# Expert loads in the order of use, and the branch to the general path ahead of the last two units

## The chip, the cores and the metric

The kernel runs on one core of a Trainium2 chip. The metric is the device time of one execution in microseconds. A core has engines that run their own instruction streams and wait for each other by semaphores: TensorE (PE, with PEld for its weight loads), VectorE (DVE), ScalarE (ACT), GpSimd (POOL) and SyncE (SP), which here issues every load from HBM. TensorE's granted clock has two levels, 1.2 and 2.4 GHz; the profile gives its mean as a share of the higher one.

## The reference

Two transformer blocks of two layers each work on 256 tokens of width 1024. Each layer is a token mixer and then a mixture of experts with 32 experts, of which every token uses two: first the best of four groups, then the two best of its eight experts. Cut to what matters, for block 1 (`D_EXPERT` is 512; in block 2 it is 256 and a layer norm takes the place of the gate):

```python
def hier_moe(h, wg, bg, we, be, w1, w3, w2):
    ...                                   # router: two experts and two weights per token
    xb = xt[buf_tok].reshape(nblk, MOE_BLOCK, d)   # tokens gathered by expert
    def expert_block(args):
        xi, e = args
        hid = jax.nn.silu(xi @ w1[e]) * (xi @ w3[e])
        return hid @ w2[e]
    yb = lax.map(expert_block, (xb, blk_exp)).reshape(p_rows, d)
    return zeros.at[buf_tok].add(yb * buf_w[:, None])
x = x + mixer(norm(x))
x = x + gt_f * hier_moe(modulate(norm(x)), ...)
```

All 32 experts' weights are read in every layer, in float32.

## The kernel before, in words

The program is one straight list of instructions, traced in Python; a scheduler then puts them in an order on each engine by its own costs and by the dependencies, and the result is fixed when the program is built. There are four expert stages: two in block 1 (`centred` false in the function `moe`) and two in block 2 (`centred` true), each behind a mixer.

In a stage the experts are taken in 11 units: five of two experts with room for 64 tokens each, five of four experts with room for 32, and a last one of two. The first 4 (block 1) or 6 (block 2) experts have fixed places; the rest is ordered by how many tokens chose them, so their weights' addresses are known only when the router is done. SP reads the order into a register (`TENSOR_LOAD kidx`, L726).

For each unit, with the names of the trace:
- `s<-w,xg` (L981): the gathered tokens `xg` times the joined w1 and w3 (tensor A), eight blocks k of the inner dimension. In block 1 a unit does this in two steps, half of its experts each.
- `hid` (L986, L987): SiLU on ACT, product on DVE; transposed on PE (L998) and copied by ACT to `ht` (L1000).
- `s<-w,ht` (L905, function `second`): `hid` times w2 (tensor B), for output half 0 and then half 1.
- `yh`, `yl` (L907 on ACT, L908 on DVE): the result in two parts for two cheaper products.
- `y<-yh,PT` and `y<-yl,PT` (L918, function `combine`): adds to the tokens' sums in PSUM. `back` prepares `PT`.
- `ms<-P,x` (L851): gathers the next group's tokens.

Weights pass through a ring of slots of 128 x 2048 float32, 1 MB each, filled by SP (L170). In block 1 the ring has 13 slots and 9 more during the expert stage; in block 2 it has 13 and 5. An expert takes four slots for A and two for B in block 1, two for A and one for B in block 2. A load may start when the products that read the slot's old contents are done. In before a unit's experts come one after the other, each with all its parts; then come the B parts. A product over block k needs the part with that k of every expert of its step; `second` of half 0 needs only the first half of each B.

A general path (`overfull`) stands for the case that an expert has more tokens than room. It is behind a branch on a count (`tc.If`, L740, its register loads on L965) and is not taken in these runs. No instruction traced behind the branch runs ahead of it on any engine, and SP waits there until its outstanding loads have landed. In before the branch stands inside the last unit. The path adds its result straight into `x` (block 1) or into `keep`, the residual sum (block 2). `residual` makes `keep`: in block 1 the gate row, in block 2 the sum of x and the scaled residual by four DVE operations (L1895, L1896) that need two `lnp` loads.

Of the kernel before, what the change touches and what calls it, by code (L numbers as in the profile page):

```python
# [28 lines left out]
E = 32  # L29
CAP = 64  # L30
# [21 lines left out]
class Core:  # L52
# [124 lines left out]
    def slot(self, src, shape):  # L177


        n = int(np.prod(shape[1:]))  # L180
        parts = -(-n // SLOT)
        m = n // parts
        views = []
        for i in range(parts):
            v = self.scratch()[:, :m]
            d = self.load(v, src[:, i * m:(i + 1) * m])
            if self.ordered:
                self.loaded = d.ins
            views.append(v.rearrange("p (a b) -> p a b", b=shape[2]) if len(shape) == 3 else v)
        return Blocks(views, shape) if parts > 1 else views[0]  # L190


class Blocks:
# [591 lines left out]
def moe(c, ctx, index, scale, shift, w13, w2, nf, spare, centred, residual, end):  # L785
# [150 lines left out]
    def experts(unit):  # L936
        e0, ne, _ = unit
        return [e0 + i if e0 < fixed else ranks.expert(e0 + i) for i in range(ne)]

    for g, us in enumerate(groups):  # L940
        if g:
            P, xg = nxt[:2]
        nxt = group(groups[g + 1], False) if g + 1 < len(groups) else (None, None, [])
        share = -(-len(nxt[2]) // len(us))
        for unit in us:
            e0, ne, cap = unit
            j = e0 - us[0][0]
            last = unit is units[-1]
            todo = [nxt[2].pop(0) for _ in range(min(share, len(nxt[2])))]
            pr = {"n": units.index(unit), "unit": unit, "h": []}  # L950
            who = experts(unit)
            if last:

                room, hT, keep = [c.scratch(), c.scratch()], c.scratch(), c.scratch()
                hT = hT.rearrange("p (a b) -> p a b", b=256)
                out, gate = residual(mp, keep, room)
                c.ordered = True
                slots = [w13(e) for e in who]
                pr["w2"] = [w2(e) for e in who]
                c.loaded, c.ordered = None, False  # L960
            pr["yh"] = p.tile([128, 2, 512], F32R, name="yh", tag="yy", bufs=2)
            pr["yl"] = p.tile([128, 2, 512], F32R, name="yl", tag="yy", bufs=2)

            def spare_path():
                n = nc.values_load(cnt[0:1, 0:1], min_val=0, max_val=E * CAP,  # L965
                                   skip_runtime_bounds_check_because="counts of tokens")
                overfull(c, sp, None if centred else c.tok, scale, shift, out, w, pos, n, nf, *spare, gate, room, hT, ranks)

            if last and centred:
                second(prev, 0)  # L970
                spare_path()
            per = ne // steps_of
            for u in range(steps_of):
                ws = slots[u * per:u * per + per] if last else [w13(e) for e in who[u * per:u * per + per]]
                q = sp.tile([128, 512], F32, name="s1")
                for k in range(8):
                    for i in range(128 // cap):

                        m, o = (i, 0) if centred else (i // 2, i % 2)
                        e = j + u * per + m  # L980
                        d = nc.tensor.matmul(q[cap * i:cap * i + cap, :], xg[:, k, e * cap:(e + 1) * cap],  # L981
                                             ws[m][:, k, 512 * o:512 * o + 512], start=k == 0, stop=k == 7)
                        if last and u == steps_of - 1 and k == 0:
                            c.loaded = d.ins
                hid = p.tile([128, 256], F32, name="hid", bufs=2)
                nc.scalar.activation(hid, q[:, 0:256], AF.Silu)  # L986
                nc.vector.tensor_mul(hid, hid, q[:, 256:512])  # L987
                half = len(todo) // 2
                for f in todo[:half] if u == 0 else todo[half:]:
                    f()  # L990
                if last and not centred and u == 0:
                    back(pr, j)
                    combine(prev)
                elif centred and prev is not None and not last:
# [7 lines left out]
                if last and not centred and u == 0:  # L1002
                    spare_path()
            if not last:
                pr["w2"] = [w2(e) for e in who]
            if centred:
                for f in todo[half:]:
                    f()
                if prev is not None:
                    second(prev, 1)  # L1010
                back(pr, j)
                if prev is not None:
                    combine(prev)
            elif not last:
                back(pr, j)
                second(pr, 0)
                if prev is not None:
                    combine(prev)
                second(pr, 1)
            prev = pr  # L1020
    c.table(second(prev, 0))
    combine(prev, (0,))
    second(prev, 1, "s1")
    combine(prev, (1,))
    end(room, keep, y)
    c.less(extra)


# [829 lines left out]
def experts_1(c, l):  # L1858

    nc, x = c.nc, c.x  # L1860
    with ExitStack() as ctx:
        def residual(mp, keep, room):
# [3 lines left out]
            return x, keep[:, 0:1024]  # L1866

        a1 = c.a["A1"][l].rearrange("(q i) p (k c) -> q i p k c", i=2, c=1024)
        b1 = c.a["B1"][l].rearrange("(q i) p (h f c) -> q i f p h c", i=2, h=2, f=4)

        def w1_of(pr, i, j, f):
            o = (f // 2) * 512 + j * 256 + (f % 2) * 128
            return a1[bass.ds(pr, 1), i, :, :, o:o + 128].rearrange("q p k c -> p (q k) c")

        def w2_of(pr, i, f):
            return b1[bass.ds(pr, 1), i, f].rearrange("q p h c -> p (q h) c")

        def end(room, gate, y):
            for hf in range(2):
                for t in range(2):  # L1880
                    o = (2 * t + hf) * 512
                    d = room[0][:, o:o + 512]
                    nc.vector.tensor_mul(d, y[t][hf], gate[:, hf * 512:hf * 512 + 512])
                    nc.vector.tensor_add(x[:, t, hf * 512:hf * 512 + 512], x[:, t, hf * 512:hf * 512 + 512], d)
        moe(c, ctx, l, c.gain, c.mod[:, l, 24:32], lambda e: c.slot(expert(c.a["A1"][l], e), [128, 8, 1024]),
            lambda e: c.slot(expert(c.a["B1"][l], e), [128, 2, 2048]), 512, (w1_of, w2_of), False, residual, end)


def residual_2(c, lnp, l, which, out):
# [9 lines left out]
def experts_2(c, l):  # L1899

    nc, x = c.nc, c.x
    with ExitStack() as ctx:
        a2 = c.a["A2"][l].rearrange("(q i) p (k c) -> q i p k c", i=2, c=512)
        b2 = c.a["B2"][l].rearrange("(q i) p (h f c) -> q i f p h c", i=2, h=2, f=2)

        def w1_of(pr, i, j, f):
            o = j * 256 + f * 128
            return a2[bass.ds(pr, 1), i, :, :, o:o + 128].rearrange("q p k c -> p (q k) c")

        def w2_of(pr, i, f):  # L1910
            return b2[bass.ds(pr, 1), i, f].rearrange("q p h c -> p (q h) c")

        def residual(mp, keep, room):
# [7 lines left out]
        moe(c, ctx, 2 + l, c.vec("lnc")[:, o:o + 8], c.vec("lnc")[:, o + 8:o + 16],  # L1921
            lambda e: c.slot(expert(c.a["A2"][l], e), [128, 8, 512]),
            lambda e: c.slot(expert(c.a["B2"][l], e), [128, 2, 1024]), 256, (w1_of, w2_of), True, residual, end)


def last(c, p, l, keep, y):
# [314 lines left out]
```

## Time and profile before

| | |
|---|---|
| three runs | 2489.33 us median (2487.82 to 2495.08) |
| profiled execution | 2492.49 us, span 2490.7 us |
| busy: PE, PEld, DVE, ACT, POOL | 2145.9, 1235.4, 882.3, 752.5, 41.5 us |
| moved by DMA | 775.10 MB, mean 311 GB/s |
| loads `w<-A`, `w<-B` | 384 and 192 of 1024.0 KB |
| mean granted clock | 0.927 |

The times come from three runs, the rows from one profiled execution. The span is from the first to the last instruction. Busy shares are means over mixers and expert stages, which have different limits, so the windows by stage are to be read instead: one row gives the busy time of each engine in a stretch, the clock, the share of the 16 DMA engines and the rate. The four expert stages lie at about 297 to 773, 947 to 1421, 1694 to 1951 and 2226 to 2477 us. In a timeline the bracket says how long the engine was idle and what ended that.

### The profile page before, as it was taken

The numbers are of one execution on the slowest core, as the hardware profiler recorded it, in microseconds if no ns is written. First come the engines' busy times: TensorE is split into PE (matmuls) and PEld (weight loads), VectorE is DVE, ScalarE is ACT, GpSimd is POOL, SyncE is SP. The second block draws the span as 40 slices with busy tenths as digits, with TensorE's granted clock in tenths as the row PEclk, the third lists the DMA queues.
The fourth block names the chain that finished last, engine by engine and source line by source line (L and its number), as shares of the span: only waits on it lengthen the run. The fifth ranks groups of instructions, "written<-read, shape, count | busy, mean of one in ns | idle before, by whom it ended". The sixth has DMA issues, their size and how long they took to land. (4 is left out here: it accounts for less than half of the span.)

```text
span 2490.7 us, 32411 instructions
## 1 busy us (share of the span) xinstructions
PE 2145.9 (86%) x12546; PEld 1235.4 (50%) x12546; DVE 882.3 (35%) x1979; ACT 752.5 (30%) x1493; POOL 41.5 (2%) x46
## 2 busy tenths in 40 slices
PE   7998899966668989997666699998987899999976
PEld 4667544322225864442221287994432678964322
DVE  3865511100003752111000254973111547851203
ACT  4642322211114451121111254562221445632211
POOL 0001000000001200000000000000000000000000
PEclk8999999988888998999888899998998889989998
DMA  9976669999997355999999951555899724557995
GB/s 394 402 279 263 252 272 401 421 421 421 421 421 309 120 235 186 402 412 421 421 421 422 390 200 58 200 188 231 344 422 418 316 87 139 187 193 288 422 420 228
DMA packets 110627, 775.10 MB, mean 311 GB/s; under 512 B 13161, under 2 KB 14569, under 8 KB 18042
## 3 DMA queue, kind: packets, MB, share of 16 engines
q1 hardware_dynamic: 110458, 772.85, 77.2%
q8 instruction: 106, 1.74, 0.3%
q14 instruction: 63, 0.52, 0.1%
HBM read 771.75 MB, written 1.05 MB: 310 GB/s over the span
## 5 line engine op out<-in xcount | busy, mean ns | idle before, releaser
L981 PE MATMUL s<-w,xg 128*32 128x512 f32 (+1 forms) x3072 | 603.2, 644 | 101.2 <-DMA w<-A 91.7
L905 PE MATMUL s<-w,ht 128*32 128x512 f32 (+1 forms) x1536 | 339.4, 663 | 64.1 <-DMA w<-B 63.1
L981 PEld LDWEIGHTS s<-w,xg 128*32 128x32 f32 (+1 forms) x3072 | 143.8, 127 | 410.5 <-issue 250.4
L369 PE MATMUL pj<-hi,wh 128*128 128x256 f32 x864 | 244.1, 285 | 3.4 <-ACT sg L1771 2.3
L370 PE MATMUL pj<-lo,wh 128*128 128x256 f32 x864 | 243.4, 283 | 0.0
L371 PE MATMUL pj<-hi,wl 128*128 128x256 f32 x864 | 240.6, 284 | 0.0
L908 DVE SCALAR_TENSOR_TENSOR yl<-s,ws,yh 128x512 fp32r<-128x512 f32 x88 | 66.0, 750 | 471.8 <-ACT yh L907 468.1
L905 PEld LDWEIGHTS s<-w,ht 128*32 128x32 f32 (+1 forms) x1536 | 84.4, 128 | 240.8 <-issue 142.5
L364 ACT ACTIVATE wh<-w 128x512 fp32r<-128x512 f32 x248 | 154.2, 630 | 120.0 <-PE pj L370 87.6
L907 ACT ACTIVATE yh<-s,ws 128x512 fp32r<-128x512 f32 x88 | 60.5, 688 | 419.4 <-PE s L905 405.8
L365 DVE TENSOR_TENSOR wl<-w,wh 128x512 fp32r<-128x512 f32 x248 | 167.2, 688 | 50.2 <-ACT wh L364 44.9
L987 DVE TENSOR_TENSOR hid<-hid,s 128x256 f32<-128x256 f32 x66 | 27.7, 420 | 439.1 <-ACT hid L986 439.1
L369 PEld LDWEIGHTS pj<-hi,wh 128*128 128x128 f32 x864 | 165.8, 192 | 10.5 <-ACT sg L1771 2.8
L986 ACT ACTIVATE hid<-s 128x256 f32<-128x256 f32 x66 | 25.4, 384 | 478.0 <-PE s L981 477.7
L371 PEld LDWEIGHTS pj<-hi,wl 128*128 128x128 f32 x864 | 164.4, 192 | 4.5 <-issue 1.4
L370 PEld LDWEIGHTS pj<-lo,wh 128*128 128x128 f32 x864 | 166.2, 192 | 0.7 <-issue 0.7
L332 DVE TENSOR_TENSOR wl<-w,wh 128x512 fp32r<-128x512 f32 (+2 forms) x164 | 112.6, 695 | 99.2 <-ACT wh L331 82.6
L331 ACT ACTIVATE wh<-w 128x512 fp32r<-128x512 f32 (+2 forms) x164 | 99.8, 614 | 115.1 <-PE pj L317 58.0
L851 PEld LDWEIGHTS ms<-P,x 128*128 128x128 f32 x640 | 80.6, 190 | 62.6 <-ACT xg L859 32.0
L859 ACT ACTIVATE xg<-ms,mod,gain 128x128 f32<-128x128 f32 x160 | 72.1, 458 | 125.4 <-PE ms L851 124.8
L317 PE MATMUL pj<-wl,hi 128*128 128x512 f32 (+2 forms) x272 | 106.9, 394 | 0.0
L316 PE MATMUL pj<-wh,hi 128*128 128x512 f32 (+2 forms) x272 | 102.2, 404 | 3.0 <-ACT rt L385 1.6
(636 smaller groups left out, 2723.9 us busy)
## 6 DMA issues: line engine op xcount, KB each, us to landing
w<-A SPq DMA_DIRECT2D x384, 1024.0 KB, 19.7
w<-B SPq DMA_DIRECT2D x192, 1024.0 KB, 19.7
w<-ada SPq DMA_DIRECT2D x48, 1024.0 KB, 9.1
w<-wi SPq DMA_DIRECT2D x48, 1024.0 KB, 8.6
w<-w SPq DMA_DIRECT2D x26, 1024.0 KB, 15.1
w<-wo SPq DMA_DIRECT2D x16, 1024.0 KB, 5.2
w<-wbr SPq DMA_DIRECT2D x8, 1024.0 KB, 5.0
w<-wi SPq DMA_DIRECT2D x4, 840.0 KB, 4.8
```

What stands on the lines that cost most here:

```text
L316: nc.tensor.matmul(qs[t][:, :n], a, wh[:, :n], start=s, stop=False)
L317: nc.tensor.matmul(qs[t][:, :n], a, wl[:, :n], start=False, stop=False)
L331: nc.scalar.activation(wh[:, :n], w[:, k], AF.Copy)
L332: nc.vector.tensor_sub(wl[:, :n], w[:, k], wh[:, :n].bitcast(F32))
L364: nc.scalar.activation(wh, w[:, k], AF.Copy)
L365: nc.vector.tensor_sub(wl, w[:, k], wh.bitcast(F32))
L369: nc.tensor.matmul(d, wh[:, e], hi, start=k == 0 and ch % 2 == 0, stop=False, skip_group_check=True)
L370: nc.tensor.matmul(d, wh[:, e], lo, start=False, stop=False, skip_group_check=True)
L371: nc.tensor.matmul(d, wl[:, e], hi, start=False, stop=k == nk - 1, skip_group_check=True)
L851: nc.tensor.matmul(q, src[i][:, t, k * 128:(k + 1) * 128], P[:, t, :m], start=start and t == 0, stop=stop and t == 1, skip_group_check=True)
L905: nc.tensor.matmul(q[cap * i:cap * i + cap, :], ht[:, o * cap:o * cap + cap], pr["w2"][i][:, half, f * 512:f * 512 + 512], start=f == 0, s ...
L981: d = nc.tensor.matmul(q[cap * i:cap * i + cap, :], xg[:, k, e * cap:(e + 1) * cap], ws[m][:, k, 512 * o:512 * o + 512], start=k == 0, sto ...
```

## The change

Three things are done in `moe`; line numbers of the changed kernel are 27 to 47 higher in the parts quoted.

First, `slots` replaces `slot` for the experts: the parts of all experts of a step are loaded in turn, part 0 of each, then part 1 of each. For B the two output halves come in turn in the same way. In block 2, where a B fits one slot with both halves, two experts' pieces of the same half now share a slot, as two DMAs of 512 KB; and a unit's B is loaded behind the next unit's A (`outer(prev, ...)`).

Second, the branch and its preparations stand at the unit `turn = len(units) - 2`, behind the loads of that unit's first step. In block 2 the unit before is finished completely ahead of it (`second` twice and `combine`).

Third, in block 1 the general path adds into a slot of its own (`held`, zeroed by GpSimd), which two DVE additions add to `x` in the last two units. `keep` and `held` are taken out of the ring.

```diff
+    def slots(self, srcs, shape):
+        n = shape[1] * shape[2]
+        parts = -(-n // SLOT)
+        views = [[] for _ in srcs]
+        for i in range(parts if parts > 1 else shape[1]):
+            for j, src in enumerate(srcs):
+                if parts > 1:
+                    v, m = self.scratch(), SLOT
+                else:
+                    m = shape[2]
+                    if j % (SLOT // m) == 0:
+                        room = self.scratch()
+                    v = room[:, j % (SLOT // m) * m:(j % (SLOT // m) + 1) * m]
+                d = self.load(v, src[:, i * m:(i + 1) * m])
...
+    def hold(self, pools):
+        pool = next(r for r in self.rings if r in pools)
+        self.rings.remove(pool)
+        return pool.tile([128, SLOT], F32, name="w")
...
+    def first(who, u):
+        per = len(who) // steps_of
+        return c.slots([w13(e) for e in who[u * per:u * per + per]], [128, 8, 512 if centred else 1024])
+    def outer(pr, who):
+        pr["w2"] = c.slots([w2(e) for e in who], [128, 2, 4 * nf])
+    turn = len(units) - 2
...
+            if n == turn:
+                if centred and prev is not None:
+                    outer(prev, experts(prev["unit"]))
+                    second(prev, 0)
+                    second(prev, 1)
+                    combine(prev)
+                    prev = None
+                keep = c.hold(extra)
+                held = None if centred else c.hold(extra)
+                begun = first(who, 0)
+                room, hT = [c.scratch(), c.scratch()], c.scratch()
+                out, gate = residual(mp, keep, room, held)
+                count = nc.values_load(cnt[0:1, 0:1], min_val=0, max_val=E * CAP,
+                                       skip_runtime_bounds_check_because="counts of tokens")
+                overfull(c, sp, None if centred else c.tok, scale, shift, out, w, pos, count, nf, *spare, gate, room,
+                         hT, ranks)
...
-                ws = slots[u * per:u * per + per] if last else [w13(e) for e in who[u * per:u * per + per]]
+                ws = begun if begun is not None and u == 0 else first(who, u)
...
-                if last and not centred and u == 0:
-                    spare_path()
-            if not last:
-                pr["w2"] = [w2(e) for e in who]
+            if last and not centred:
+                for t in range(2):
+                    nc.vector.tensor_add(c.x[:, t], c.x[:, t], out[:, t])
...
+    if centred:
+        outer(prev, prev["who"])
     c.table(second(prev, 0))
     combine(prev, (0,))
     second(prev, 1, "s1")
     combine(prev, (1,))
-    end(room, keep, y)
+    end(held, keep, y)
```

SP's list at the end of the first stage, before: the last unit's A and B loads, the branch, then the next mixer's loads (`A1` and `B1` are the weights of block 1, the numbers are slots in the order in which they are taken).

```order
L170 DMA w_4698<-A1 128x2048
...
L170 DMA w_4700<-B1 128x2048
...
L170 DMA w_4706<-B1 128x2048
L965 TENSOR_LOAD rcnt_2662
L740 COMPARE_AND_BRANCH
...
L740 UNCONDITIONAL_BRANCH
L170 DMA w_5286<-w1b 128x128
```

The same place in the changed kernel: eight A loads of the tenth unit, the branch, and behind it the rest of that unit and all of the last, then the mixer's loads.

```order
L170 DMA w_4453<-A1 128x2048
L1004 TENSOR_LOAD rcnt_2662
L767 COMPARE_AND_BRANCH
...
L767 UNCONDITIONAL_BRANCH
L753 TENSOR_LOAD kidx_2627
...
L170 DMA w_4926<-A1 128x2048
...
L170 DMA w_5003<-B1 128x2048
...
L170 DMA w_5154<-B1 128x2048
...
L170 DMA w_5156<-B1 128x2048
L170 DMA w_5302<-w1b 128x128
```

Behind the branch stand 16 A loads and 12 B loads, 28 in all, where none stood; the branch is no longer between the experts' loads and the mixer's.

PE's list behind the branch of the first stage, before (`s_5134` the last unit's second s1 step, `s_5159` and `s_5175` its two output halves):

```order
L740 UNCONDITIONAL_BRANCH
L998 MATMUL ms<-ident,hid 128x128 x2
L981 MATMUL s_5134<-w,xg 64x512 x16
L905 MATMUL s_5159<-w,ht 64x512
L998 MATMUL ms<-ident,hid 128x128 x2
L905 MATMUL s_5175<-w,ht 64x512
L905 MATMUL s_5159<-w,ht 64x512 x7
L905 MATMUL s_5175<-w,ht 64x512 x7
L918 MATMUL y<-yh,PT 128x512 x2
L918 MATMUL y<-yl,PT 128x512 x2
L918 MATMUL y<-yh,PT 128x512 x2
```

The end of the same stage on PE in the changed kernel (`s_5123` the same s1 step, `s_5175` and `s_5191` the halves); the branch stands 27 rows earlier.

```order
L1023 MATMUL s_5123<-w,xg 64x512 x16
L932 MATMUL s_5175<-w,ht 64x512
L1036 MATMUL ms<-ident,hid 128x128 x2
L957 MATMUL ms<-ident,Pw 128x128 x2
L932 MATMUL s_5175<-w,ht 64x512 x7
L932 MATMUL s_5191<-w,ht 64x512
L945 MATMUL y<-yh,PT 128x512 x2
L945 MATMUL y<-yl,PT 128x512 x2
L932 MATMUL s_5191<-w,ht 64x512 x7
L945 MATMUL y<-yh,PT 128x512 x2
```

The arithmetic of the last unit is the same; what moved is the branch, and the first half's `y` products stand ahead of most of the second half's. The trace counts two matmuls for each one in these lists where the operands are plain float32.

DVE's list around the branch of the third stage, before: the four residual operations (L1895, L1896) stand ahead of one more `hid` and `yl` and the branch.

```order
L908 SCALAR_TENSOR_TENSOR yl<-s_13516,ws,yh 128x512
L1895 SCALAR_TENSOR_TENSOR w<-x,w 128x1024 x2
L1896 SCALAR_TENSOR_TENSOR w<-w 128x1024 x2
L987 TENSOR_TENSOR hid<-hid,s_13406 128x256
L932 TENSOR_SCALAR PT<-ms 128x256
L934 TENSOR_REDUCE ws<-ms 128x1
L908 SCALAR_TENSOR_TENSOR yl<-s_13574,ws,yh 128x512
L965 TENSOR_LOAD rcnt
L740 COMPARE_AND_BRANCH
```

In the changed kernel they stand directly ahead of it, behind the last `yl` of the ninth unit.

```order
L935 SCALAR_TENSOR_TENSOR yl<-s_13392,ws,yh 128x512
L935 SCALAR_TENSOR_TENSOR yl<-s_13458,ws,yh 128x512
L935 SCALAR_TENSOR_TENSOR yl<-s_13469,ws,yh 128x512
L1942 SCALAR_TENSOR_TENSOR w<-x,w 128x1024 x2
L1943 SCALAR_TENSOR_TENSOR w<-w 128x1024 x2
L1004 TENSOR_LOAD rcnt
L767 COMPARE_AND_BRANCH
...
L767 UNCONDITIONAL_BRANCH
L1027 TENSOR_TENSOR hid<-hid,s_13726 128x256
```

Their `lnp` loads stand on SP as the last two ahead of the branch in the changed kernel, and in before eleven loads earlier, ahead of the tenth unit's last A load. The products `s_13726` of the tenth unit are the first on PE behind the branch.

## Rows read from the trace of the kernel before

**Rows 1.** The page's 40 slices, rate of the DMA in each.
```profile
GB/s 394 402 279 263 252 272 401 421 421 421 421 421 309 120 235 186 402 412 421 421 421 422 390 200 58 200 188 231 344 422 418 316 87 139 187 193 288 422 420 228
```

**Rows 2.** --windows of two stages: length, busy time of each engine, clock, DMA share, GB/s.
```profile
425.00:750.00 325.00, 237.28 (x1388) 79.50 (x1384) 32.06 (x86) 42.03 (x91) 0.30 (x1) 0.89 1.01 421
1775.00:1930.00 155.00, 128.74 (x725) 47.19 (x723) 25.12 (x47) 29.01 (x56) 0.00 (x0) 0.94 1.01 421
```

**Rows 3.** Groups of 425 to 750: busy, mean ns, idle before and its releasers.
```profile
L981 PE MATMUL s<-w,xg 128*32 128x512 f32 x640 | 93.0, 648 | 35.1 <-DMA w<-A 35.1
L905 PE MATMUL s<-w,ht 128*32 128x512 f32 x320 | 63.1, 740 | 31.4 <-DMA w<-B 31.2
```

**Rows 4.** DMA issues, two answers: count, KB each, us to landing.
```profile
w<-A SPq DMA_DIRECT2D x36, 1024.0 KB, 19.7
...
w<-lnp SPq DMA_DIRECT2D x2, 512.0 KB, 18.0
...
cols<-cols SPq DMA_DIRECT2D x1, 76.0 KB, 1.9
```

**Rows 5.** Timeline behind the branch, first stage: start, us, engine, line, instruction, idle before.
```profile
750.58 10.08 PE L981 MATMUL s<-w,xg 128*64 128x512 f32 x32 [4.73 <-DVEq L740]
...
757.20 0.35 SPq L170 DMA_DIRECT2D w<-w1b  x1
...
761.95 7.62 PE L905 MATMUL s<-w,ht 128*64 128x512 f32 x30
...
771.91 0.73 PE L918 MATMUL y<-yl,PT 128*128 128x512 f32 x2 [0.76 <-DVE yl L908]
```

**Rows 6.** The same of the second stage.
```profile
1405.03 0.82 SPq L170 DMA_DIRECT2D w<-wi  x2
...
1420.85 0.73 PE L918 MATMUL y<-yl,PT 128*128 128x512 f32 x2 [0.73 <-DVE yl L908]
```

**Rows 7.** The same of the third stage (first of block 2).
```profile
1903.89 2.36 DVE L1895 SCALAR_TENSOR_TENSOR w<-x,w 128x1024 f32<-128x1024 f32 x2 [8.88 <-DMA w<-lnp]
1904.06 7.60 PE L981 MATMUL s<-w,xg 128*32 128x512 f32 x50
...
1906.17 2.35 DVE L1896 SCALAR_TENSOR_TENSOR w<-w 128x1024 f32<-128x1024 f32 x2
...
1927.73 0.76 PE L918 MATMUL y<-yl,PT 128*128 128x512 f32 x1 [6.04 <-PEq L740]
...
1930.33 3.64 PE L905 MATMUL s<-w,ht 128*32 128x512 f32 x16
...
1933.17 0.82 SPq L170 DMA_DIRECT2D w<-wi  x2
...
1934.47 3.65 PE L981 MATMUL s<-w,xg 128*64 128x512 f32 x16
...
1950.23 0.72 PE L918 MATMUL y<-yl,PT 128*128 128x512 f32 x2
```

**Rows 8.** --windows around the four branches.
```profile
745.00:770.00 25.00, 19.74 (x70) 7.57 (x71) 1.51 (x4) 3.51 (x6) 2.74 (x3) 0.80 0.81 320
1395.00:1415.00 20.00, 15.20 (x57) 5.68 (x57) 0.42 (x1) 1.15 (x3) 0.15 (x1) 0.83 0.82 326
1925.00:1945.00 20.00, 16.08 (x60) 4.86 (x62) 1.72 (x4) 1.46 (x3) 0.00 (x0) 0.77 0.83 329
2445.00:2463.00 18.00, 11.31 (x44) 2.80 (x40) 1.69 (x3) 1.38 (x2) 0.00 (x0) 0.72 0.82 328
```

**Rows 9.** --windows where loads wait for slots, stages one and three.
```profile
375.00:400.00 25.00, 25.00 (x115) 10.50 (x113) 4.43 (x14) 5.49 (x13) 0.00 (x0) 1.00 0.97 397
1711.00:1776.00 65.00, 63.86 (x293) 27.11 (x294) 12.78 (x32) 16.44 (x32) 0.00 (x0) 0.97 0.70 277
```

**Rows 10.** Line 740 (the branch) on DVE: duration ns min/median/max, first and last start.
```profile
L740 DVEq COMPARE_BRANCH  x4: 56/68/72, 744.5 to 2447.5; - x4
...
L740 DVEq EVENT_SEMAPHORE  x4: 21/21/21, 750.3 to 2448.0; - x4
```

More of the change, by code (lines that the diff above doesn't have):

```diff
@@ L190, in slot @@
         return Blocks(views, shape) if parts > 1 else views[0]
+    def slots(self, srcs, shape):
[12 more added lines that the diff above has]
+                d = self.load(v, src[:, i * m:(i + 1) * m])
+                if self.ordered:
+                    self.loaded = d.ins
+                views[j].append(v.rearrange("p (a b) -> p a b", b=shape[2]))
+        return [Blocks(v, shape) for v in views]
+    def hold(self, pools):
+        pool = next(r for r in self.rings if r in pools)
+        self.rings.remove(pool)
+        return pool.tile([128, SLOT], F32, name="w")
 class Blocks:
@@ L947, in moe @@
             j = e0 - us[0][0]
-            last = unit is units[-1]
+            n = units.index(unit)
+            last = n == len(units) - 1
             todo = [nxt[2].pop(0) for _ in range(min(share, len(nxt[2])))]
-            pr = {"n": units.index(unit), "unit": unit, "h": []}
+            pr = {"n": n, "unit": unit, "h": []}
             who = experts(unit)
+            begun = None
+            if n == turn:
[9 more added lines that the diff above has]
+                room, hT = [c.scratch(), c.scratch()], c.scratch()
+                hT = hT.rearrange("p (a b) -> p a b", b=256)
+                out, gate = residual(mp, keep, room, held)
[3 more added lines that the diff above has]
+                         hT, ranks)
+                c.loaded = None
+                who = experts(unit)
@@ L952, in moe @@
             if last:
-                room, hT, keep = [c.scratch(), c.scratch()], c.scratch(), c.scratch()
-                hT = hT.rearrange("p (a b) -> p a b", b=256)
-                out, gate = residual(mp, keep, room)
                 c.ordered = True
-                slots = [w13(e) for e in who]
-                pr["w2"] = [w2(e) for e in who]
-                c.loaded, c.ordered = None, False
             pr["yh"] = p.tile([128, 2, 512], F32R, name="yh", tag="yy", bufs=2)
             pr["yl"] = p.tile([128, 2, 512], F32R, name="yl", tag="yy", bufs=2)
[L964 to L967, printed above, removed]
@@ L980, in moe @@
                         e = j + u * per + m
[L981 to L984, printed above, removed]
+                        nc.tensor.matmul(q[cap * i:cap * i + cap, :], xg[:, k, e * cap:(e + 1) * cap],
+                                         ws[m][:, k, 512 * o:512 * o + 512], start=k == 0, stop=k == 7)
                 hid = p.tile([128, 256], F32, name="hid", bufs=2)
@@ L990, in moe @@
                     f()
-                if last and not centred and u == 0:
-                    back(pr, j)
-                    combine(prev)
-                elif centred and prev is not None and not last:
+                if centred and prev is not None:
+                    outer(prev, prev["who"])
                     second(prev, 0)
@@ L1001, in moe @@
                 pr["h"].append(ht)
-                if last and not centred and u == 0:
-                    spare_path()
-            if not last:
-                pr["w2"] = [w2(e) for e in who]
+            pr["who"] = who
+            if last and not centred:
+                for t in range(2):
+                    nc.vector.tensor_add(c.x[:, t], c.x[:, t], out[:, t])
             if centred:
@@ L1013, in moe @@
                     combine(prev)
-            elif not last:
+            else:
+                outer(pr, who)
                 back(pr, j)
-                second(pr, 0)
-                if prev is not None:
+                if last:
                     combine(prev)
-                second(pr, 1)
+                else:
+                    second(pr, 0)
+                    if prev is not None:
+                        combine(prev)
+                    second(pr, 1)
             prev = pr
+    if centred:
+        outer(prev, prev["who"])
+    c.ordered = False
     c.table(second(prev, 0))
@@ L1861, in experts_1, with residual @@
     with ExitStack() as ctx:
-        def residual(mp, keep, room):
+        def residual(mp, keep, room, held):
             dg = room[0][:, 0:512].rearrange("p (a b) -> p a b", b=128)
@@ L1865, in residual @@
                 rows(c, dg, mp, c.mod[:, l, 40 + 4 * hf:44 + 4 * hf], keep[:, hf * 512:hf * 512 + 512], tag=("ms", 2))
-            return x, keep[:, 0:1024]
+            nc.gpsimd.memset(held, 0.0)
+            return held.rearrange("p (t d) -> p t d", t=2), keep[:, 0:1024]
         a1 = c.a["A1"][l].rearrange("(q i) p (k c) -> q i p k c", i=2, c=1024)
@@ L1881, in end @@
                     o = (2 * t + hf) * 512
-                    d = room[0][:, o:o + 512]
+                    d = room[:, o:o + 512]
                     nc.vector.tensor_mul(d, y[t][hf], gate[:, hf * 512:hf * 512 + 512])
                     nc.vector.tensor_add(x[:, t, hf * 512:hf * 512 + 512], x[:, t, hf * 512:hf * 512 + 512], d)
-        moe(c, ctx, l, c.gain, c.mod[:, l, 24:32], lambda e: c.slot(expert(c.a["A1"][l], e), [128, 8, 1024]),
-            lambda e: c.slot(expert(c.a["B1"][l], e), [128, 2, 2048]), 512, (w1_of, w2_of), False, residual, end)
+        moe(c, ctx, l, c.gain, c.mod[:, l, 24:32], lambda e: expert(c.a["A1"][l], e),
+            lambda e: expert(c.a["B1"][l], e), 512, (w1_of, w2_of), False, residual, end)
 def residual_2(c, lnp, l, which, out):
@@ L1911, in w2_of, with residual @@
             return b2[bass.ds(pr, 1), i, f].rearrange("q p h c -> p (q h) c")
-        def residual(mp, keep, room):
+        def residual(mp, keep, room, held):
             out = keep.rearrange("p (t d) -> p t d", t=2)
@@ L1921, in experts_2 @@
         moe(c, ctx, 2 + l, c.vec("lnc")[:, o:o + 8], c.vec("lnc")[:, o + 8:o + 16],
-            lambda e: c.slot(expert(c.a["A2"][l], e), [128, 8, 512]),
-            lambda e: c.slot(expert(c.a["B2"][l], e), [128, 2, 1024]), 256, (w1_of, w2_of), True, residual, end)
+            lambda e: expert(c.a["A2"][l], e),
+            lambda e: expert(c.a["B2"][l], e), 256, (w1_of, w2_of), True, residual, end)
 def last(c, p, l, keep, y):
```

2 lines of the change are left out of this document (removed).

## The prediction

> **What bounds the kernel now.** I read the 40 slices first: the rate stands at about 421 GB/s for many slices in each of the four expert stages and nowhere else for long [rows 1]. The windows say it in one number each: over 325 us of the first stage and 155 us of the third the share is 1.01 and the rate 421, with PE busy 237 of 325 and 129 of 155 us at a mean granted clock of 0.89 and 0.94 [rows 2]. The groups of the first window name what PE's idle time ends on: `w<-A` 35.1 us and `w<-B` 31.4 us [rows 3]. So in the second half of each stage a 1 MB load costs 1.0486/0.421 = 2.49 us and nothing else matters. A load takes 19.7 us to land because eight are outstanding, 8 x 2.49 [rows 4]. Two things stand outside this. Behind the last load of a stage the rest of the arithmetic is bare: I call this the tail. And early in the stages of block 2 PE is full (63.86 of 65 us) and the rate is 277 [rows 9], so there the loads wait for slots.
>
> **The change, term by term.** The sum is made against the profiled execution: 2492.49 us, span 2490.7. It lies 3.2 above the median of 2489.33. Times are per stage; T is where SP goes on behind the branch, which is where the last load has landed.
>
> *Tail of block 1's stages.* SP resumes at 757.20 and the last y product ends at 771.91 + 0.73 = 772.64: 15.4 us [rows 5]. In layer 1 it is 1405.03 to 1421.58: 16.5 [rows 6]. It is long because the last unit's s1 products start at 750.58 only (PE waited 4.73 for DVE to pass the branch), last 10.08, and most of both output halves follows (7.62). In the changed order the branch stands before the last two units, and the last two loads are the second output half alone. Left behind T: half of one half's 16 products, 8 x 0.254 = 2.0 us (0.254 = 7.62/30), then 3.07 from the end of the products (761.95 + 7.62 = 769.57) to 772.64, plus about 1 for landing and start: 6.2. Without that 1, or at twice the time for the products, 5.1 to 8.2. Gain: 15.4 - 6.2 and 16.5 - 6.2, together 19.5. It needs PE to have caught up by then; between branch and end stand 28 loads, 70 us of DMA, and PE is busy for 73% of such time [rows 2], so it has.
>
> *The drain.* At the branch SP waits until every load has landed, then the queue starts empty. In before that hole lies behind the last expert load; in after it lies in the middle. Lost time by the rate in the windows around the four: 25 x (1 - 320/421) = 6.0, 20 x (1 - 326/421) = 4.5, 20 x (1 - 329/421) = 4.4, 18 x (1 - 328/421) = 4.0 [rows 8]. The first has small loads behind it, so 4.4 each is taken; bounds 4.0 and 6.0. All later loads, the end T with them, move by that: +4.4 x 4 = 17.6.
>
> *Order of loads, block 1.* What it can give back is time the queue lost while slots were held: 25 x (1 - 397/421) = 1.4 just behind the first fill, and as much one unit later [rows 9]; before that two more slots could come free by half a unit, 2 x 2.49 = 5. I take 1.5 per stage from 0 to 5: -3.0 for two. The slot zeroed on GpSimd and two DVE additions (like the two that took 2.36 us in [rows 7]) lie beside DMA time: 0; bare they would be 2.5.
>
> *Order, block 2.* Lost here: 65 x (1 - 277/421) = 22 us [rows 9], but PE is full in it, so most of it only restates that PE is slow there. What the order frees: the w2 parts come one unit later, so 2 to 4 slots do not lie idle for a unit, 5 to 10 us of loads issued ahead. Against that two slots fewer are filled ahead of the order numbers (16 instead of 18), up to 5 us. Bounds 0 and 10; I take 5, the lower end of the slot count: -10 for two. That w2 comes in 512 KB pieces I put at 0 to 1 us; `lnp` pieces of that size land in 18.0 beside 19.7 [rows 4].
>
> The Trainium skill ("DMA: Bandwidth & Descriptors", Rules for kernel authors) asks for 1 MiB or more per DMA where bandwidth is wanted, which speaks against halves. The trace has 2.49 us from load to load with eight in flight, so that cost does not show here [rows 2, 4]; what it would be if it did is a rival below.
>
> *Tail of block 2's stages.* In before PE ends 1950.23 + 0.72 - 1933.17 = 17.8 us behind T, with the branch beside the last loads: on PE it shows as 6.04 before the y product [rows 7]. In after PE's pipeline is emptied ahead of the branch, and PE's own branch is hidden in the drain. But DVE's four residual operations (2.36 + 2.35 us) wait for `lnp`, the last load of the drain, and stand ahead of DVE's branch. Queued behind that branch is everything that frees the bank of the next s1 product. How long DVE's branch takes has two answers: the first of the four from 744.5 to 750.3, 5.8 us, and the last from 2447.5 to 2448.0, 0.5 us [rows 10]. The last is the one of block 2, whose general path is the shorter, so 0.5 is taken and 5.8 kept as bound. PE goes on 3.7 + 0.5 + 0.6 = 4.8 us behind the drain's end (one residual operation can run on the first `lnp` half, three are left). PE's work from there: s1 of a four-expert unit 64 x 0.152 = 9.7 (7.60/50); gathers 4; s1 of the last unit 32 x 0.228 = 7.3 (3.65/16); two second products of 3.64 and the last unit's two halves in 3.65, 11 [rows 7]; y products and transposes about 7; bare waits 2; 41 in all. Loads from there: 10 slots, 25 us, and the hole, 29.3. So PE ends 4.8 + 41 - 29.3 = 16.5 behind the last load, about 16 where gathers overlap: -2 per stage, -4 for two. Bounds: 21 (+3) with DVE's branch at 5.8, and 28 (+10) if all 41 run at a clock near 0.77 [rows 8].
>
> *Sum.* -19.5 + 17.6 - 3.0 - 10 - 4 = -18.9; with 1 for the smaller pieces -18. 2492.5 - 18 = 2474.5 in the profile, 2471 as median.
>
> **The rivals.**
> A. The order gives all it can: 5 per stage in block 1, 10 in block 2. -19.5 + 17.6 - 10 - 20 - 4 = -36: 2453. For it: in both stretches of [rows 9] slots are what a load waits for. Against: PE is full in them and sets the pace.
> B. The order gives nothing, since PE hands out the slots anyway, and DVE's branch takes 5.8 in block 2 as well: -19.5 + 17.6 + 6 = +4: 2493, no change. For it: 63.86 of 65 us, and two of the four branches that I can place in [rows 10] differ.
> C. Slower: PE stands empty through the drain of block 2 (20 us) and 4.8 more, and comes back at a low clock, as 32 products took 10.08 us behind the branch [rows 5] where 16 took 3.65 later [rows 7], so 7.3. If the clock stays near 0.77 to the end of the stage, that is +10 per stage; and if the idle PE frees no slots as well, the order gives nothing: -19.5 + 17.6 + 20 = +18: 2507. With no gain from the order it decides from +5 per stage. For it: clocks of 0.72 to 0.83 around the branches [rows 8]. Against: in before 50 products took 7.60 and 16 took 3.65 just beside the branch.
> D. The small pieces pay a fixed cost each. The 32 w2 loads of a layer become 64 pieces; at the 1.9 us that a load of 76 KB took to land on an idle queue [rows 4], all of it unhidden, the 32 more cost 61 us a layer, +122: 2611. [...] Against: eight pieces in flight are 10 us of bytes, which covers 2.
>
> **How the numbers follow.** Forecast 0.47, A 0.17, B 0.20, C 0.14, D 0.02. A measurement here can tell 0.3%, 7.5 us: faster means under 2481.9, slower over 2496.8. The forecast's own range is 2460 to 2483 (block 1 -9 to -4 a stage, block 2 -6 to -1 with the bounds of 4.0 and 6.0 on the hole), so 0.42 of it is faster and 0.05 no change. Faster 0.42 + 0.17 + 0.03 from B = 0.62; same 0.05 + 0.17 = 0.22; slower 0.14 + 0.02 = 0.16. The range reaches to A below and to B above, and leaves out C, D and the far end of A: 2453 to 2494.
>
> **What would show it.** In after, the last y product of block 1 ends about 6 us behind the last load instead of 15 and 16; the window of 20 us just behind each branch has a rate near 325; no branch stands behind the last load. In block 2 PE is idle some 20 us around the branch, DVE's branch takes 0.5 us, and the last y product comes about 16 behind the last load. The forecast is wrong if PE lags in block 1's tails, if the hole at a branch exceeds 6 us, or if the rate in the stretch of block 2 where PE is full does not rise above 277.

## The result

The changed kernel took 2465.4 us (median of 4 runs, 2457.6 to 2467.93) against 2491.14 before: a ratio of 0.9891, 95% interval 0.9863 to 0.9919. That is 26 us less; the forecast of 2471 is 20 below 2491, with a range of 2453 to 2494. Measured a second time beside other runs (e5 below) it took 2463.06, ratio 0.9893 (0.9878 to 0.9908). The profiled execution is the fastest of its runs (2457.6 us, span 2455.8), so the two profiles lie further apart, 34.9 us, than the medians.

The rate in 40 slices of the profile after, for [rows 1]:

```profile
GB/s 393 407 272 284 219 271 400 422 421 422 421 384 419 112 207 255 369 401 421 421 421 383 421 288 47 190 196 223 377 417 379 370 86 142 189 155 356 414 417 234
```

The 421 stands in the same places, but a slice of 383 or 384 has come into the first and second stage: the drain at the branch, now in the middle. Windows of 25 us at each of the four branches (columns as in [rows 8]):

```profile
675.00:700.00 25.00, 18.04 (x100) 6.29 (x100) 0.42 (x1) 1.93 (x5) 0.00 (x0) 0.74 0.81 328
1310.00:1335.00 25.00, 14.92 (x81) 4.76 (x80) 0.61 (x2) 1.22 (x3) 0.00 (x0) 0.76 0.81 327
1870.00:1895.00 25.00, 8.81 (x64) 2.49 (x64) 4.63 (x4) 0.01 (x1) 0.00 (x0) 0.61 0.85 343
2388.00:2413.00 25.00, 8.64 (x64) 2.52 (x64) 4.63 (x4) 0.00 (x0) 0.00 (x0) 0.59 0.85 334
```

Lost are 25 x (1 - 328/421) = 5.5, then 5.6, 4.6 and 5.2 us. In the last two windows PE is busy for under 9 of 25 us: it stands empty. Two windows that answer to [rows 9], at about the same distance from the stage's first s1 product (76 for 78 us in stage one, 11 for 10 in stage three):

```profile
375.00:400.00 25.00, 25.00 (x116) 10.22 (x114) 4.35 (x14) 4.76 (x11) 0.00 (x0) 1.00 1.01 421
1695.00:1760.00 65.00, 64.04 (x294) 28.53 (x292) 12.36 (x31) 17.43 (x33) 0.00 (x0) 0.97 0.96 372
```

In the third stage the rate while PE is full rose from 277 to 372, so 14.7 us of loads run earlier: 65 x (372 - 277)/421. The ends of the stages of block 1, to be read beside [rows 5] and [rows 6], first stage one and then two:

```profile
756.70 3.65 PE L932 MATMUL s<-w,ht 128*64 128x512 f32 x16 [0.84 <-DMA w<-B]
...
762.59 3.65 PE L932 MATMUL s<-w,ht 128*64 128x512 f32 x14
...
767.80 0.74 PE L945 MATMUL y<-yl,PT 128*128 128x512 f32 x2
```

```profile
1394.74 3.65 PE L932 MATMUL s<-w,ht 128*64 128x512 f32 x16 [0.87 <-DMA w<-B]
...
1405.84 0.73 PE L945 MATMUL y<-yl,PT 128*128 128x512 f32 x2
```

The bracket at 756.70 is the second load of output half 0; two loads of 2.49 stand behind it, so the last lands near 761.6, and the last y product ends at 768.54: 6.9 us. In stage two it is 1394.74 + 4.98 and 1406.57: 6.9 again, where 15.4 and 16.5 stood before. Around the branch of the third stage, beside [rows 7]:

```profile
1881.10 2.36 DVE L1942 SCALAR_TENSOR_TENSOR w<-x,w 128x1024 f32<-128x1024 f32 x2 [16.23 <-DMA w<-lnp]
1883.34 2.79 SPq L170 DMA_DIRECT2D w<-A  x4
1883.38 2.35 DVE L1943 SCALAR_TENSOR_TENSOR w<-w 128x1024 f32<-128x1024 f32 x2
...
1886.04 8.81 PE L1023 MATMUL s<-w,xg 128*32 128x512 f32 x64 [20.38 <-DVEq L767]
...
1924.33 0.74 PE L945 MATMUL y<-yl,PT 128*128 128x512 f32 x2
```

PE waits 20.38 us for DVE to pass the branch, and DVE waits for `lnp`. From 1886.04 PE works to 1925.07 with 2 us of gaps (busy 37.05 us of 1886 to 1925); the last w2 piece landed at 1913.39, so the tail is 11.7 where 17.8 stood before.

A stage is measured from its first s1 product to the end of its last y product. Nine of the profiles, in us; the stages of e4, e5 and e8 stand in their paragraphs:

| stage | before | after | e1 order alone | e2 branch alone | e3 no branch | e6 | e7 | e9 | e10 |
|---|---|---|---|---|---|---|---|---|---|
| 1 | 475.3 | 469.2 | 466.3 | 472.6 | 463.5 | 467.4 | 467.4 | 476.5 | 469.6 |
| 2 | 477.1 | 467.9 | 469.6 | 472.0 | 465.0 | 469.4 | 469.4 | 476.9 | 469.4 |
| 3 | 250.2 | 241.4 | 235.3 | 248.5 | 235.1 | 245.8 | 241.2 | 236.8 | 243.6 |
| 4 | 248.0 | 241.4 | 237.2 | 250.8 | 234.6 | 244.1 | 239.9 | 236.6 | 242.8 |
| median of the runs | 2491 | 2465.4, 2463.1 | 2450.6 | 2488.8 | 2439.5 | 2468.4 | 2458.6 | 2467.6 | 2469.5 |

By stage the change gained 6.1, 9.2, 8.8 and 6.6 us, 30.8 of the 34.9 between the profiles; the mixers between have the rest.

### The profile page after: what moved, and what is told of

Same layout as the page of the kernel before. It is cut to its first block, busy times and chain, and to the rows that moved or that the text cites. A ratio compares the mean times of both kernels' runs of the same rounds, so it can differ in the third digit from the quotient of the medians.

```text
span 2455.8 us, 32737 instructions
## 1 busy us (share of the span) xinstructions
PE 2159.5 (88%) x12546; PEld 1229.3 (50%) x12546; DVE 886.6 (36%) x1983; ACT 749.9 (31%) x1493; POOL 44.6 (2%) x48
## 5 line engine op out<-in xcount | busy, mean ns | idle before, releaser
L1023 PE MATMUL s<-w,xg 128*32 128x512 f32 (+1 forms) x3072 | 612.8, 627 | 94.9 <-DMA w<-A 53.7
L932 PE MATMUL s<-w,ht 128*32 128x512 f32 (+1 forms) x1536 | 348.8, 603 | 38.5 <-DMA w<-B 37.3
L396 PEld LDWEIGHTS pj<-hi,wh 128*128 128x128 f32 x864 | 164.9, 191 | 10.4 <-ACT sg L1817 2.8
## 6 DMA issues: line engine op xcount, KB each, us to landing
w<-A SPq DMA_DIRECT2D x384, 1024.0 KB, 17.7
```

The costliest lines, as they stand in the source:

```text
L396: nc.tensor.matmul(d, wh[:, e], hi, start=k == 0 and ch % 2 == 0, stop=False, skip_group_check=True)
L932: nc.tensor.matmul(q[cap * i:cap * i + cap, :], ht[:, o * cap:o * cap + cap], pr["w2"][i][:, half, f * 512:f * 512 + 512], start=f == 0, s ...
```

## The experiments

Each ran beside the kernel before on the same chip; the ratio is to that. e1 to e4 share one set of runs, e5 to e8 a second, e9 and e10 a third. The table above has the stages.

**e1, the order alone.** The kernel before with the new loads; the branch stays in the last unit.

```diff
-                slots = [w13(e) for e in who]
-                pr["w2"] = [w2(e) for e in who]
+                slots = sum([first(who, u) for u in range(steps_of)], [])
+                outer(pr, who)
...
-                ws = slots[u * per:u * per + per] if last else [w13(e) for e in who[u * per:u * per + per]]
+                ws = slots[u * per:u * per + per] if last else first(who, u)
```

> The new order of loads (parts in turn, w2 of block 2 one unit later) with the branch left in the last unit. Theory: the order lets loads run ahead while PE is full, about 19 us over the four stages, and the tails stay at 15 to 19 us behind the last load: about 2471 us where before has 2490 and the changed kernel 2465. Rival 1, the order alone is the whole gain: 2465. Rival 2, only the place of the branch counts, the order is paced by PE: 2490.

Measured: 2450.57, ratio 0.9833 (0.9819 to 0.9847). It is 13 to 15 us faster than the changed kernel: my theory and both rivals named nothing below 2465. The order is more than the whole gain, and the tails shorten without any move of the branch. DVE behind the branch of stage one in before, and then the end of that stage in e1, beside [rows 5]:

```profile
750.42 0.17 DVE L1993 SCALAR_TENSOR_TENSOR gain<-mod,cols 128x8 f32<-128x8 f32 x1 [6.10 <-DVEq L740]
```

```profile
740.75 0.66 PE L1030 MATMUL ms<-ident,hid 128*128 128x128 f32 x2 [4.85 <-PEq L761]
...
742.85 0.17 DVE L2026 SCALAR_TENSOR_TENSOR gain<-mod,cols 128x8 f32<-128x8 f32 x1 [6.05 <-DVEq L761]
...
743.00 8.85 PE L1012 MATMUL s<-w,xg 128*64 128x512 f32 x32 [1.59 <-DVE gain L2026]
...
753.69 7.08 PE L926 MATMUL s<-w,ht 128*64 128x512 f32 x30 [0.47 <-ACT ht L1032]
...
754.56 0.35 SPq L170 DMA_DIRECT2D w<-w1b  x1
...
763.11 0.73 PE L939 MATMUL y<-yl,PT 128*128 128x512 f32 x2 [0.74 <-DVE yl L929]
```

SP resumes at 754.56 and the last y product ends at 763.84: 9.3 us where 15.4 stood; in stage two it is 10.4 where 16.5 stood. PE meets its six microseconds at the branch here too (4.85 of them idle), but relative to the last load it is through 4.9 us earlier: DVE goes on 754.56 - 742.85 = 11.7 ahead of SP, where before it was 757.20 - 750.42 = 6.8. The 32 products then take 8.85 against 10.08 us, at a granted clock of 0.80 (743 to 752) against 0.70 (750.5 to 760.7).

**e2, the branch alone.** The changed kernel with the old order of loads.

```diff
-        for i in range(parts if parts > 1 else shape[1]):
-            for j, src in enumerate(srcs):
+        for j, src in enumerate(srcs):
+            for i in range(parts):
...
+            if centred:
+                outer(pr, who)
```

> The branch ahead of the last two units with its own slot, but experts loaded one after the other and w2 right behind its unit as in before. Theory: tails shorter by 6 to 10 us per stage (-31 in all), the hole of the drain moved into the middle (+20): about 2479. Rival 1, the order is the whole gain: 2490 or above. Rival 2, only the place counts: 2465.

Measured: 2488.82, ratio 0.9986 (0.9976 to 0.9995): 3 us, where I had 12. Stages one and two gain 3 to 5 us, three 2, and four loses 3. The sum is small because two effects of opposite sign are in it. The end of stage one in e2:

```profile
760.71 7.97 PE L928 MATMUL s<-w,ht 128*64 128x512 f32 x30
...
771.03 0.73 PE L941 MATMUL y<-yl,PT 128*128 128x512 f32 x2 [0.73 <-DVE yl L931]
```

The last load lands near 764.0 (the one before it at 761.50), so the tail is 7.8 us where 15.4 stood; in stage two it is 8.1 (1409.03 to 1417.16). So the move of the branch does shorten these tails, in the old order too. But the last load lands 5.0 and 3.5 us later behind the stage's first product. That is the drain: 25 us at the two branches have 326 and 325 GB/s (680 to 705 and 1325 to 1350), so 5.6 and 5.7 us are lost. In sum the place of the branch is worth little with the old order, and with the new order it costs: 2450.6 with the branch late, 2463.1 and 2465.4 with it early.

**e3, no branch.** The changed kernel without the count and the call of `overfull`.

> The changed kernel without the branch and the general path behind it (left out: the case of an expert with more tokens than room, which does not occur here). Theory: no drain, so the last load of each stage lands 4.4 to 6 us earlier, and in block 2 PE is not emptied, so the tail there is 7 instead of 12: 2465 - 20 - 10 = about 2435 to 2440. Rival: the hole is refilled since PE has a backlog that decides the end, then 2460.

Measured: 2439.53, ratio 0.9785 (0.977 to 0.98), within the forecast. Against the changed kernel stages one to four are 5.7, 2.9, 6.3 and 6.8 shorter, 22 in all: this is what the early branch costs. Against e1 they are 2.8, 4.6, 0.2 and 2.6 shorter: the late branch costs about 10, most of it in block 1, as far as e1 and e3 are otherwise alike.

**e4, lnp earlier.** The two `lnp` loads of block 2 ahead of the tenth unit's A loads.

```diff
-                begun = first(who, 0)
+                begun = None if centred else first(who, 0)
...
                 out, gate = residual(mp, keep, room, held)
+                if centred:
+                    begun = first(who, 0)
```

> The changed kernel with the two lnp loads of block 2 ahead of the tenth unit's A loads instead of behind them. Theory: DVE's four residual operations run during the drain, the first s1 products behind the branch start about 3 us earlier, and PE's tail in block 2 is 3 us shorter per stage: about 2459. Rival, PE is not what ends block 2's stages (the last loads are): no change, 2465.

Measured: 2458.86, ratio 0.9863 (0.9847 to 0.988). The total is as forecast, 4 to 6 us better, but the intervals of the two ratios touch, and the stages say less: against e5 (469.3, 469.4, 241.4, 241.2) stage three stays (241.7), four gains 2.7 (238.5), and 2.3 come from block 1, which the edit doesn't touch. In stage three PE does go on much earlier, at 1875.80, 12 us ahead of SP's 1887.95, where in the changed kernel it went on 2.7 behind; against the first profile the tail is 9.8 instead of 11.7, but the last load lands 2.2 us later, and why was not found. What the edit is worth is not settled.

**e5, the changed kernel again**, beside e6 to e8.

> The changed kernel once more, unaltered, beside the same runs of before as the next three. It says whether the gap of 15 us between it (2465.4) and the order alone (2450.6) is real. If the branch ahead of two units costs its drain: 2462 to 2468. If the first four runs of it were slow by chance: about 2450.

Measured: 2463.06, ratio 0.9893 (0.9878 to 0.9908). The interval does not meet that of e1: the gap is real.

**e6, w2 of block 2 in its old place.** e1 with `outer(pr, who)` at the end of the own unit.

```diff
-                if centred:
-                    outer(prev, experts(prev["unit"]))
...
-                    outer(prev, prev["who"])
...
-            if not last and not centred:
+            if not last:
                 outer(pr, who)
```

> The order alone, but in block 2 the w2 pieces again right behind their own unit's w13. Revised theory: this part frees slots in block 2 while PE is full (rate 277 there before, 371 with the order alone); without it the last loads of block 2 land 2.4 to 6 us later: about 2459 to 2462. Rival, w13 in turn is all of the gain: 2451.

Measured: 2468.36, ratio 0.9916 (0.9902 to 0.9929). More than forecast: 18 us of e1's 41 hang on the late w2. Nearly all of it is in block 2 (+10.5 and +6.9; block 1 has +1.1 and -0.2). The last loads are 6.1 and 4.7 us later, near the upper end of what I had, and the tails are 4.3 and 2.1 longer, which I did not have. What it does is seen while PE is full, 1700 to 1765 in stage three, e6 and then e1:

```profile
1700.00:1765.00 65.00, 65.00 (x295) 27.46 (x295) 10.28 (x22) 17.94 (x34) 0.00 (x0) 0.97 0.80 302
```

```profile
1700.00:1765.00 65.00, 65.00 (x294) 26.66 (x294) 10.70 (x23) 17.63 (x33) 0.00 (x0) 0.98 0.97 373
```

With PE at 65 of 65 us in both, the rate is 302 and 373. The edit changes only where w2 stands, so I take it that the slots which a w2 holds for a unit are what the loads wait for; which slot each load waited for was not followed.

**e7, w13 expert by expert.** e1 with the parts of each expert's w13 together again.

```diff
-        return c.slots([w13(e) for e in who[u * per:u * per + per]], [128, 8, 512 if centred else 1024])
+        return [c.slots([w13(e)], [128, 8, 512 if centred else 1024])[0] for e in who[u * per:u * per + per]]
```

> The order alone, but w13 expert by expert as in before (w2 in halves in turn and late as in the order alone). Revised theory: with parts in turn PE can start a unit when the first part of each expert has landed, so it lags less behind the loads, its granted clock stays up and the tails are 6 to 9 us shorter; without it 2475 to 2480. Rival, the place of w2 is the larger part: 2460 or less.

Measured: 2458.6, ratio 0.9868 (0.9853 to 0.9883): 8 us, a third of what I expected, and again in block 2 only (+5.9, +2.7). That w13 in turn shortens the tails of block 1 is refuted. The granted clock did go down without it, 0.94 over 425 to 650 us where e1 has 0.98, but the stages of block 1 hardly changed (+1.1 and -0.2 us).

**e8, the branch at the fourth unit.**

```diff
-    turn = len(units) - 2
+    turn = 3
```

> The changed kernel with the branch at the fourth unit instead of the tenth. Theory: there PE is full and loads wait for slots anyway, so the drain costs the last load little: 2448 to 2456. Rival, the drain takes away the lead of the loads wherever it stands, and the one or two slots kept out of the ring for longer add to it: 2465 to 2475.

Measured: 2475.47, ratio 0.9941 (0.9928 to 0.9955), the upper end of the rival. Stages of 475.0, 471.7, 244.0 and 244.1. The tails are short, 5.6 to 7.0 us, so the loss is all in the last loads, which land 4 to 9 us later than in the changed kernel. A drain while PE is full was not free here. How much of it is the drain and how much the slots held out of the ring was not separated.

**e9, w2 of block 1 expert by expert.** e1 with each w2's two halves together in block 1.

```diff
+        if centred:
+            pr["w2"] = c.slots([w2(e) for e in who], [128, 2, 4 * nf])
+        else:
+            pr["w2"] = [c.slots([w2(e)], [128, 2, 4 * nf])[0] for e in who]
```

> The order alone, but in block 1 each expert's w2 again as a whole, half 0 and half 1, before the next expert's. Theory: in block 1 it is the halves in turn that matter: half 0 of a unit of four can start after four loads instead of seven, so PE lags three loads (7.5 us) less at the branch and the tail is 6 shorter; undone, both stages of block 1 go back from 466 to 470 to about 475 and the whole to 2463 to 2467. Rival, w13 in turn does it in block 1 together with the halves: 2451 to 2456.

Measured: 2467.59, ratio 0.9907 (0.9894 to 0.992). As the theory had it: block 1 is back at 476.5 and 476.9, block 2 as in e1. Of the 17.5 us that block 1 loses, 12 are tail (15.9 and 16.3 us against 9.4 and 10.7) and 5 are last loads that land later. The second products of the tenth unit in stage one, before and then e1, whose stages began at 297.3 and 297.5:

```profile
718.41 1.28 PE L905 MATMUL s<-w,ht 128*32 128x512 f32 x2 [3.53 <-DMA w<-B]
...
723.38 6.56 PE L905 MATMUL s<-w,ht 128*32 128x512 f32 x26 [3.69 <-DMA w<-B]
...
732.40 3.64 PE L905 MATMUL s<-w,ht 128*32 128x512 f32 x32
```

```profile
713.69 3.62 PE L926 MATMUL s<-w,ht 128*32 128x512 f32 x26 [1.10 <-DMA w<-B]
...
718.92 1.05 PE L926 MATMUL s<-w,ht 128*32 128x512 f32 x4
...
723.62 3.62 PE L926 MATMUL s<-w,ht 128*32 128x512 f32 x26 [1.43 <-DMA w<-B]
```

In before the bulk of half 0 ends at 729.94, and half 1 follows at 732.40 to 736.04, though only one load, 2.49 us, stands between the last of half 0 and the last of half 1. In e1 half 0 ends at 717.31 and half 1 at 727.24. So PE is done with this unit 8.8 us earlier, and DVE comes to the branch at 737.0 instead of 744.5. The six microseconds there then lie beside loads that are still on the way: the last A load of the last unit landed at 745.8 in before, 4.8 us ahead of the products that read it (750.58), and at 744.5 in e1, 1.5 us behind their start (743.00).

**e10, the branch at the last unit** with its own slot.

```diff
-    turn = len(units) - 2
+    turn = len(units) - 1
```

> The changed kernel with the branch and its preparations at the last unit instead of the last but one (behind that unit's first A loads, own slot, pipeline of block 2 emptied ahead). Theory: the drain ahead of the last load costs the same 2.5 to 5.5 us wherever it stands, so block 1 stays at 468 to 469 a stage; in block 2 only 4 A and 4 half loads are left behind it while PE has some 22 us of work, so the tail there grows to about 16: about 2473. Rival, the price goes with the number of loads behind the branch: 2452 to 2458.

Measured: 2469.53, ratio 0.9909 (0.9896 to 0.9923). Block 1 is at 469.6 and 469.4, as in the changed kernel: a stage is as long with 8 loads behind the branch as with 28 (the last load lands 0.9 and 0.8 us earlier, the tail is 1.3 and 2.3 longer). Block 2 is 2.2 and 1.4 longer, and not by its tail as I had it: in stage three that is 9.8 instead of 11.7, and the last load lands 4.1 us later. The price does not go with the number of loads behind the branch.

e6, e7 and e9 each undo one part of e1, and 18 + 8 + 17 = 43 against its gain of 41 (46 when each is set against the kernel before in its own runs). With intervals of 3 to 4 us on each, the three parts account for the gain and nearly add up; what each would bring without the others was not run.

## Why the prediction came out, and where it was wrong

The time was right, 2471 for 2465 (or 2463), but partly by luck: an effect of the order is missing from the sum, and it falls almost wholly on tails that the sum had already booked under the branch. By stage the sum has -13.7 for block 1 and -5 for block 2; measured are -15.3 and -15.4.

A stage is the time from its first s1 product to the landing of its last expert load, plus the tail from there to its last y product. The traces give both, in us (the tails count from the landing, which is 0.1 to 1.1 ahead of SP's next load; where that landing is not marked it is SP's wait for it, or one load's time behind the load before):

| stage | before | e2 branch alone | e1 order alone | after |
|---|---|---|---|---|
| 1 | 459.8 + 15.5 | 464.8 + 7.8 | 456.9 + 9.4 | 462.2 + 7.0 |
| 2 | 460.3 + 16.8 | 463.8 + 8.1 | 458.9 + 10.7 | 460.9 + 7.0 |
| 3 | 231.4 + 18.8 | 234.3 + 14.2 | 225.7 + 9.6 | 229.7 + 11.7 |
| 4 | 230.3 + 17.7 | 236.9 + 13.9 | 227.5 + 9.7 | 229.8 + 11.5 |
| all, less before | | +18.0 and -24.8 | -12.8 and -29.4 | +0.8 and -31.6 |

*The branch:* the drain was put at +17.6, the tails at -19.5 and -4. With the branch alone moved (e2) it is +18.0 and -24.8. These terms and their mechanism are right, the tails of block 1 included: 6.2 forecast, 7.8 and 8.1 in e2, 7.0 in the changed kernel. The holes in the windows are 4.6 to 5.6 where I had 4.4, bounds 4.0 to 6.0.

*The order, as loads issued earlier:* -3 and -10 forecast; with the order alone (e1) the last loads land 4.3 earlier in block 1 and 8.5 in block 2. Right as well.

*The order, and PE's lag:* here a step failed. "What it can give back is time the queue lost while slots were held" lets the order act on the loads only, and so does the term for block 2; what it does to PE, and so to the tails, was put at nothing without a reason. With the branch where it was, the order takes 29.4 us from the tails, 12.2 in block 1 and 17.2 in block 2. In block 1 that is PE coming late to the branch because half 0 of the unit before had to wait for seven of its eight w2 loads (e9).

*The sum:* the branch takes 24.8 from the tails, the order 29.4, both together 31.6 and not 54. I read the wait of 4.73 us at the branch [rows 5] as the one cause of the long tail. There are two, and it is bare only while both are there: an early PE covers the branch's six microseconds with loads, and a branch ahead of the last two units is not met at the end. So behind the new order the early branch wins 2 us of tail and pays 13.6 us in the last loads. By the medians it loses 13 to 15 us against the late branch (e1), and by stage 22 against none (e3).

*Order, block 2:* rival A's "slots are what a load waits for" was the better reading. Its "PE is full and sets the pace", on which rival B stood, is refuted: PE is as full as before at a rate of 372, and with w2 in its old place the rate is 302 (e6).

*Tail of block 2:* 16 forecast, 11.7 measured. PE went on 2.7 us behind the drain where I had 4.8 (1886.04 - 1883.34), worked 39.0 us where I had 41, and the loads took 30.1 where I had 29.3. Three errors of 0.8 to 2.1 us with one sign. DVE's branch was 1.9 us in the last stage (2402.2 to 2404.1 below), between my 0.5 and the bound of 5.8.

```profile
L767 DVEq COMPARE_BRANCH  x4: 56/68/72, 672.2 to 2402.2; - x4
L767 DVEq EVENT_SEMAPHORE  x4: 21/21/21, 677.9 to 2404.1; - x4
```

*Rivals C and D* did not decide. The granted clock is 0.50 while PE stands empty (1870 to 1886), but 0.80 over the next 9 us and 0.95 over 1886 to 1925, and the 64 products from 1886.04 took 8.81 us where I had 9.7. With 512 KB pieces in flight beside the 1 MB loads the rate is 417 GB/s, which the next window of stage three shows.

```profile
1760.00:1865.00 105.00, 100.17 (x595) 37.65 (x593) 18.61 (x39) 23.59 (x47) 0.00 (x0) 1.00 1.02 417
```

The Trainium skill ("DMA: Bandwidth & Descriptors", Rules for kernel authors) asks for 1 MiB or more per DMA for the most bandwidth, which speaks against halves. With eight loads in flight this run has 417 against 421 GB/s, so the measurement shows no price above 1% here.

A version that beats both kernels is e1: the order without the move of the branch, 2450.6 us.

## What to carry to other kernels

Load in the order in which parts are used, down to the output half: where the engine that computes waits for the last part of the last expert, it lags by all parts in front, and that lag is what lies bare at the end. A wait at a branch can have two causes, the branch and the lateness of the engine that meets it. Undo the candidates one at a time and then together, since what two of them win on the same tail does not add. In this kernel the branch that drains the load queue cost least behind the last load of its stage, where the queue has nothing more to bring: about 10 us over the four stages, against 22 ahead of the last two units.

## What the runs showed of the hardware that was not expected

The time an engine takes at the branch, with the general path not entered, depends on the engine and the place. The branch instruction takes PE 5.9 to 6.2 us in before, e1, e2 and the changed kernel (5.4 to 6.2 in e8), and SP and ACT 0.05:

```profile
L767 PEldq COMPARE_BRANCH  x4: 6052/6082/6208, 672.2 to 2384.2; - x4
```

On DVE the instruction takes 0.07, but from its start to the next one it is 5.5 to 5.8 us in block 1 of before, e1 and the changed kernel, and in block 2 0.4 and 0.5 (before) or 1.9 (e1, changed kernel); in e8, with the branch at the fourth unit, it is 0.4 to 0.6 in both blocks. Why is open. And the order of loads alone changes PE's granted clock while loads are the bound: over 425 to 650 us, with the same 421 GB/s, it is 0.91 before and 0.98 in e1, and 0.94 and 0.93 when w13 (e7) or w2 (e9) is loaded expert by expert again.

```profile
425.00:650.00 225.00, 171.44 (x1038) 60.19 (x1034) 23.45 (x64) 31.93 (x71) 0.00 (x0) 0.91 1.01 421
```

```profile
425.00:650.00 225.00, 187.17 (x1046) 62.09 (x1046) 24.74 (x68) 33.02 (x72) 0.00 (x0) 0.98 1.01 421
```
